# Six projection blocks in seven half-size products, with weight sums added up by loads and scan operands read from DRAM

## The chip, the cores and the metric

The kernel runs on one core of a Trainium2 chip. The metric is the device time of one execution in microseconds: the median of three runs of the kernel before is 1147.17 us (1144.52 to 1148.08).

## The reference

One decoder block works on 1024 tokens of 1024 features, in float32. It normalises the input (`h`), multiplies it by one wide weight `w_in`, and feeds two mixers from the columns of the result.

```
h = _rmsnorm(x, norm_w[layer])
proj = h @ w_in[layer]
dsa_qkv, dsa_z, gdn_qkv, gdn_z, gdn_b, gdn_a, gate_a, gate_b = _split_columns(proj)
y_a = (o_a * jax.nn.silu(dsa_z)) @ w_up_a[layer]
y_b = (o_b * jax.nn.silu(gdn_z)) @ w_up_b[layer]
merged = jax.nn.sigmoid(gate_a) * y_a + jax.nn.sigmoid(gate_b) * y_b
x = x + merged @ w_out[layer]
```

Mixer A is a mixture of three dilated window attentions (`o_a`). Mixer B is a gated delta rule, evaluated in 16 chunks of 64 tokens with a state that is handed from chunk to chunk (`o_b`):

```
v_new = u_c - jnp.einsum('bhck,bhkv->bhcv', w_c, state)
o = jnp.einsum('bhck,bhkv->bhcv', q_e, state) + jnp.einsum('bhij,bhjv->bhiv', at, v_new)
state = state * dec[..., None, None] + jnp.einsum('bhck,bhcv->bhkv', k_d, v_new)
```

A final normalisation follows. `z` (the `dsa_z` and `gdn_z` columns, 512 each) and the gates (1024 each) are plain projections of `h`.

## The kernel before

**Numbers.** Every float32 factor of a projection is held as two float16 parts (`h_hi`, `h_lo`; `whi`, `wlo`), and a product is three matmuls of float16: hi by hi, hi by lo, lo by hi (`mm3_steps`, L150 to L152). A weight block comes from DRAM in float32 (`wstage`, issued by GpSimd's queue, POOL, L132), ScalarE makes the hi part (L136) and VectorE the lo part (`wlo`, in the helper at L62).

**Units and the feed.** The projections are cut into units of 256 columns. A unit is 32 steps of three matmuls with 512 tokens each, in four outputs of 128 columns by 512 tokens. `Feed` holds the units in a row, `feed.tick(n)` writes the next n steps into TensorE's program, and while one unit runs, the weights of the next are loaded (at the start) and split (8 and 14 steps later). All other work of the kernel is written between such ticks, so that TensorE has matmuls to do while other engines prepare.

**Stages.** First `h` is made (to about 60 us), then come the attentions with the q, k and v units between them (to about 565 us), the preparation of mixer B with its units and the triangular solves (to about 790 us), the scan (to about 925 us), the up products and the output product. The solves run on VectorE at low priority, their results go through DRAM (`u_d`, `t_d`) into `MT`, and `merge` needs them.

**The scan.** Its loop (L1194) handles two chunks an iteration. A chunk has three places where TensorE needs VectorE: the state's products (L1212) go to `z` on VectorE, `z` goes into the product with `U` (L1232), its result becomes `vn` on VectorE, and `vn` goes into the state's update (L1241), which VectorE adds to `Sb`. Between them stand 4, 2 and 2 steps of the feed (`PACE`). The units that fill them are the two z units of mixer A, whose results are used at once (`z_now`), the two of mixer B (`z_keep`), and gate unit 6. Gate unit 7 is run after the scan. All operands of the scan but `kdec` lie in SBUF.

**What sets the order.** TensorE's instructions stand in the order in which the code writes them. Those of VectorE, ScalarE and the DMA queues are put in order when the kernel is built, by a scheduler that follows priorities (`tc.high_priority`, with an offset for lower ones); on the chip each engine then works off its list in that order.

## Time and profile before

| | us |
|---|---|
| median of three runs | 1147.17 |
| the profiled execution | 1144.65 |
| its span, from the first to the last instruction | 1142.9 |
| TensorE busy (PE) | 1116.6 |
| VectorE busy (DVE) | 757.9 |
| ScalarE busy (ACT) | 491.7 |

The difference of 1.75 us between execution and span lies outside of the instructions. In the rows, `out<-in` names what is written and read, `x` is a count, and a helper's line stands for all its callers (L62 and L65 are VectorE's, L150 to L152 TensorE's). A row of a timeline begins with the start and the length in us. In a table of windows a row has the stretch, its length, and then the busy time of PE, PEld, DVE, ACT and POOL, the granted clock, the share of the DMA engines and GB/s. A row of the DMA view has the count of loads, the size of one and the median time from issue to landing.

### The profile page before, as it was taken

To read this page: it belongs to the slowest core of one execution; us is meant where nothing else is said; L and a number is where in the kernel's file an instruction comes from. 1 tells how busy PE (TensorE), PEld (TensorE's weight loads), DVE (VectorE), ACT (ScalarE), POOL (GpSimd) and SP (SyncE) were. 2 spreads that over 40 slices of the span, in tenths; PEclk is the share of its full clock that TensorE was granted. 3 is DMA by queue.
4 is the path that set the end of the run, shared out by engine and by line. 5 is a ranking of instruction groups with operands and counts; after the bars stand their busy time and mean duration, and the time that the engine had idled before them with its cause. 6 is when DMAs were issued, how large, how long until landed. Compare 5 with 4: busy or idle time off the path is not lost.

```text
span 1142.9 us, 23354 instructions
## 1 busy us (share of the span) xinstructions
PE 1116.6 (98%) x9410; PEld 672.3 (59%) x9410; DVE 757.9 (66%) x1818; ACT 491.7 (43%) x1128; POOL 57.5 (5%) x103
## 2 busy tenths in 40 slices
PE   6999999999999999999999999999999999999997
PEld 6894775956857655856555544455555544444443
DVE  5775747568577378737977997973776662775223
ACT  6455746466455355446654423442322133331211
POOL 2100000000000000000000000000000000100000
PEclk9999999999999999999999999999999999999999
DMA  7144343413623423333212524242111116540232
GB/s 273 64 139 121 110 119 94 121 57 90 172 75 95 124 76 93 103 103 113 66 38 80 144 96 113 76 82 76 56 57 57 48 56 258 192 140 1 74 111 75
DMA packets 73053, 115.28 MB, mean 101 GB/s; under 512 B 30560, under 2 KB 41184, under 8 KB 72816
## 3 DMA queue, kind: packets, MB, share of 16 engines
q1 hardware_dynamic: 56064, 65.14, 19.7%
q0 software_dynamic: 12128, 44.11, 12.1%
q10 hardware_dynamic: 4752, 4.52, 1.1%
q8 instruction: 74, 1.21, 0.5%
q14 instruction: 35, 0.29, 0.1%
HBM read 73.70 MB, written 21.17 MB: 83 GB/s over the span
## 4 chain that ended last, share of the span: by engine, by line
PE 74%; DVE 18%; DMA 3%; ACT 2%; issue 2%; SPq 1%; DVEq 0%; ACTq 0%
PE ps_mm L150 20%; PE ps_mm L151 19%; PE ps_mm L152 19%; DVE wlo L62 2%; PE ps_G L607 2%; DVE ca L62 2%; DVE X L65 2%; DVE stmp L65 2%; PE ps_S L151 1%; PE ps_S L150 1%; PE ps_S L152 1%; DVE rt L65 1%; PE ps_S L586 1%; PE ps_S L584 1%; DMA og<-og 1%
## 5 line engine op out<-in xcount | busy, mean ns | idle before, releaser
L150 PE MATMUL ps_mm<-h_hi,whi 128*128 128x512 f16 (+1 forms) x912 | 345.1, 378 | 0.1
L151 PE MATMUL ps_mm<-h_lo,whi 128*128 128x512 f16 (+1 forms) x912 | 343.9, 377 | 1.0 <-DVE h_lo L65 1.0
L152 PE MATMUL ps_mm<-h_hi,wlo 128*128 128x512 f16 (+1 forms) x912 | 343.9, 377 | 0.0
L152 PEld LDWEIGHTS <-wlo 128*128 128x128 f16 x1088 | 106.4, 98 | 122.8 <-issue 1.2
L150 PEld LDWEIGHTS <-whi 128*128 128x128 f16 x1088 | 106.3, 98 | 86.3
L151 PEld LDWEIGHTS <-whi 128*128 128x128 f16 x1088 | 106.5, 98 | 79.6 <-issue 0.3
L597 ACT ACTIVATE sm<-sm,osb 128x128 f32<-128x128 f32 (+1 forms) x192 | 85.0, 444 | 91.2 <-DVE osb L593 90.6
L62 DVE SCALAR_TENSOR_TENSOR wlo<-wstage,whi 128x1024 f16<-128x1024 f32 x80 | 97.2, 1222 | 39.5 <-ACT whi L136 39.2
L150 PE MATMUL ps_mm<-whi,h_hi 128*128 128x256 f16 x384 | 105.1, 274 | 0.0
L151 PE MATMUL ps_mm<-wlo,h_hi 128*128 128x256 f16 x384 | 104.7, 273 | 0.1
L152 PE MATMUL ps_mm<-whi,h_lo 128*128 128x256 f16 x384 | 104.7, 273 | 0.0
L136 ACT ACTIVATE whi<-wstage 128x1024 f16<-128x1024 f32 x79 | 82.6, 1054 | 40.4 <-PE ps_mm L151 36.2
L65 DVE TENSOR_TENSOR tl<-ps_G,th 128x256 f16<-128x256 f32 (+1 forms) x96 | 52.1, 543 | 38.6 <-ACT th L612 38.2
L593 DVE CUSTOM_DVE_ANT_0 sm<-ps_S,amask 128x128 f32<-128x128 f32 (+1 forms) x192 | 59.4, 347 | 26.9 <-PE ps_S L586 26.8
L132 POOL DMA_DIRECT2D wstage<-in_w x68 | 36.0, 529 | 784.3 <-DVE wlo L62 594.7
L65 DVE TENSOR_TENSOR rt<-rx,tabs 128x512 f32<-128x512 f32 x96 | 64.9, 687 | 15.4 <-ACT rx L439 14.3
L62 DVE SCALAR_TENSOR_TENSOR ca<-xc,cw,ca 128x512 f32<-128x512 f32 x72 | 53.7, 746 | 2.2 <-ACT ca L793 1.6
L150 PE MATMUL ps_mm<-wo_hi,m_hi 128*128 128x512 f16 (+2 forms) x136 | 49.5, 366 | 0.0
L151 PE MATMUL ps_mm<-wo_lo,m_hi 128*128 128x512 f16 (+2 forms) x136 | 49.5, 366 | 0.0
L152 PE MATMUL ps_mm<-wo_hi,m_lo 128*128 128x512 f16 (+2 forms) x136 | 49.4, 366 | 0.0
L607 PE MATMUL ps_G<-cons,sm 128*128 128x128 f32 x280 | 46.4, 273 | 1.7 <-DVE tl L65 1.6
L151 PEld LDWEIGHTS <-h_hi 128*128 128x128 f16 x384 | 45.8, 119 | 1.3
(273 smaller groups left out, 1856.2 us busy)
## 6 DMA issues: line engine op xcount, KB each, us to landing
wstage<-in_w POOLq DMA_DIRECT2D x68, 512.0 KB, 4.6
og<-osb ACTq DMA_DIRECT2D x32, 132.0 KB, 2.1
og<-og SPq DMA_DIRECT2D x32, 132.0 KB, 2.2
gspa<-gst SPq DMA_DIRECT2D x16, 256.0 KB, 2.1
wstage<-in_w_up POOLq DMA_DIRECT2D x8, 512.0 KB, 5.0
sga<-gspa SPq DMA_DIRECT2D x8, 512.0 KB, 4.9
wstage<-in_w_out POOLq DMA_DIRECT2D x8, 512.0 KB, 4.4
xr<-in_x SPq DMA_DIRECT2D x8, 512.0 KB, 4.2
```

The lines of the kernel that those rows point to most:

```text
L62: (eng or V).scalar_tensor_tensor(out, in0, scalar, in1, op0=op0, op1=op1)
L65: (eng or V).tensor_tensor(out, in0, in1, op)
L132: (eng or nc.gpsimd).dma_start(out=st, in_=src[:, 4 * c:4 * c + 4])
L136: SC.activation(hi[:, 4 * c:4 * c + 4], st, AF.Copy, scale=W_SCALE)
L150: PE.matmul(out, lhsT=wh(k), rhs=mh(k), start=first and i == 0, stop=False, skip_group_check=True)
L151: PE.matmul(out, lhsT=wh(k), rhs=ml(k), start=False, stop=False, skip_group_check=True)
L152: PE.matmul(out, lhsT=wl(k), rhs=mh(k), start=False, stop=last and i == len(ks) - 1, skip_group_check=True)
L584: PE.matmul(out, lhsT=Q[:, hd, qs], rhs=K[:, hd, ks], start=(u == 0), stop=False, skip_group_check=True)
L586: PE.matmul(out, lhsT=Q[:, hd, qs], rhs=Kl[:, hd, ks], start=False, stop=True, skip_group_check=True)
L593: V.tensor_tensor_reduce(P[:, u, :128 * nk], psc[:, u * 256:u * 256 + 128 * nk], mask, -cexp, -NEG, ALU.add, ALU.min, accum_out=osb[:, 256 ...
L597: SC.activation(P[:, u, :128 * nk], P[:, u, :128 * nk], AF.Exp, bias=osb[:, 256 + hd:257 + hd], scale=-1.0, accum_out=osb[:, 260 + hd:261 ...
L607: PE.transpose(pt[:, c:c + 128], P[:, u, i * 128:i * 128 + 128], ident)
```

## The change

Six units are computed in another way: the four z units and the gate units 6 and 7. A unit's weight is 1024 by 256 and its tokens are 1024, so it can be seen as a product of 2 by 2 blocks, with eight products of blocks (512 deep, 128 columns, 512 tokens). The change uses a scheme with seven products of sums of blocks (`seven_products`), so a unit has 28 steps in place of 32.

- **Sums of h.** During the attentions `sums_of_h` makes the four sums of quarters of `h` on VectorE at low priority, using `kT` as scratch, and stores them in DRAM (`hs_d`). Three come back into tiles of their own (`hsum`); the fourth overwrites a quarter of `h` when gate unit 5 is done (`last_sum`).
- **Sums of weights.** Each unit's blocks lie in DRAM 14 times (`w7`). `Seven.load` loads three plain blocks into `wstage` and four into `wsum`, and then adds four, two and one further blocks to the latter with loads that accumulate (`accum_op`). `Seven.split` makes the hi and lo parts, in four parts spread over the unit before.
- **Sums of results.** They are made in PSUM: ScalarE copies a bank into another and the next product goes on top (`seed_y` and the copies beside it). One bank is kept in SBUF (`x7`), and two of the four outputs are that minus a bank, made by one more VectorE operation.
- **Scan operands.** The tiles that the scan reads (`Rv`, `q`, `U`, `at`) are spilled to DRAM when they are ready and read back iteration by iteration. `m`, `wo` and ten gate tiles become six gate tiles with the gates spilled.
- The z and up units are put into the feed earlier in the code, and the four blocks of `w_out` are fetched one in each up unit.

```diff
--- before.py
+++ after.py
+RUNS7 = 28
...
+        def ahead(self, i):
+            if i >= len(self.units):
+                return
+            at, busy, src = RUNS7 - self.left, self.seven(i - 1), self.units[i][1]
+            if not self.seven(i):
+                if not busy:
+                    self.prefetch(i, FETCH if self.left > FETCH[1] else None)
+                elif at == 1:
+                    with tc.high_priority():
+                        self.st = [load_w(src, c) for c in range(2)]
+                elif at == 17:
+                    self.w[i] = unit_tiles()
+                elif at in (18, 21):
+                    self.split(self.st[at // 21], *self.w[i], at // 21)
+            elif not busy:
+                at += RUNS - RUNS7
+                if at == 0:
+                    src.load()
+                elif at in (12, 18):
+                    src.split(at // 18)
+            elif at == 1:
+                src.load()
+            elif at in (9, 17, 25):
+                src.split(at // 8 - 1)
...
+                if self.seven(i):
+                    src = self.units[i][1]
+                    for n in range(4):
+                        src.split(n)
+                    self.cur, self.left = self.units[i][2](src.blocks), RUNS7
...
+    class Seven:
+        PAIRS = (((0, 0), (1, 0)), ((1, 2), (0, 1)), ((1, 1), (0, 2)), ((1, 3),))
+        def __init__(self, i):
+            self.src, self.blocks, self.loaded, self.split_done = A["w7"][i], [], False, 0
+        def load(self):
+            if self.loaded:
+                return
+            self.loaded = True
+            dma = nc.gpsimd.dma_start
+            with tc.high_priority():
+                self.st = [wst.tile([128, 4, 256], F32, name="wstage", tag="wstage", bufs=2)
+                           .rearrange("p a b -> p (a b)").rearrange("p (s n) -> p s n", n=512) for _ in range(2)]
+                sums = w7pool[0].tile([128, 4, 512], F32, name="wsum", tag="wsum", bufs=1)
+                dma(out=sums, in_=self.src[:, 3:7])
+                dma(out=self.st[0], in_=self.src[:, 0:2])
+                dma(out=self.st[1][:, 0:1], in_=self.src[:, 2:3])
+                dma(out=sums, in_=self.src[:, 7:11], accum_op=ALU.add)
+                dma(out=sums[:, 2:4], in_=self.src[:, 11:13], accum_op=ALU.add)
+                dma(out=sums[:, 3:4], in_=self.src[:, 13:14], accum_op=ALU.add)
+            self.sums = sums
+        def split(self, n):
+            if n < self.split_done:
+                return
+            self.load()
+            self.split_done = n + 1
+            t = w_tile(("whi", "wlo")[n % 2]).rearrange("p k c -> p (k c)").rearrange("p (b l n) -> p b l n", l=2, n=512)
+            for b, (kind, j) in enumerate(self.PAIRS[n]):
+                st = self.sums[:, j] if kind else self.st[j // 2][:, j % 2]
+                SC.activation(t[:, b, 0], st, AF.Copy, scale=W_SCALE)
+                STT(t[:, b, 1], st, W_SCALE, t[:, b, 0], ALU.mult, ALU.subtract)
+                self.blocks.append([t[:, b, x].rearrange("p (k c) -> p k c", c=128) for x in (0, 1)])
...
+    def seven_products(blocks, out):
+        x, q = bank("mm", 3), bank("mm", 3)
+        def product(n, p, first=False):
+            hi, lo = mov7[n]
+            w = blocks[n]
+            return mm3_steps(p, (lambda k: w[0][:, k], lambda k: w[1][:, k]), (hi, lo), ks=range(4), first=first)
+        def then(steps, fn):
+            for i, _ in enumerate(steps):
+                if i == 3:
+                    with tc.high_priority():
+                        fn()
+                yield
+        y, rest = [], []
+        def seed_y():
+            y.append(bank("mm", 3))
+            SC.copy(y[0], x)
+        def keep():
+            rest.append(w7pool[1].tile([128, 512], F32, name="x7", tag="x7", bufs=1))
+            SC.copy(rest[0], q)
+        yield from then(product(0, x, True), seed_y)
+        yield from then(product(1, q, True), keep)
+        yield from then(product(2, x), lambda: SC.copy(q, x))
+        yield from then(product(3, y[0]), lambda: out(0, 0, y[0], None))
+        yield from then(product(4, q), lambda: out(1, 1, q, rest[0]))
+        yield from then(product(5, x), lambda: out(1, 0, x, rest[0]))
+        yield from then(product(6, q), lambda: out(0, 1, q, None))
...
+        if rest is not None:
+            STT(t, p, -1.0, rest, ALU.mult, ALU.subtract)
+            p = t
...
+    def sums_of_h(k):
+        def halves(x):
+            return [x[:, :512], x[:, 512:]]
+        wk = [kT[2 * (k % 2) + i].rearrange("p c i -> p (c i)") for i in range(2)]
+        for i in range(2):
+            TT(wk[i], h_hi[:, 4 * i + k], h_lo[:, 4 * i + k], ALU.add)
+        (x11, x12), (x21, x22) = halves(wk[0]), halves(wk[1])
+        TT(x11, x11, x12, ALU.subtract)
+        TT(x12, x22, x12, ALU.subtract)
+        STT(x22, x22, -1.0, x11, ALU.mult, ALU.subtract)
+        STT(x21, x22, -1.0, x21, ALU.mult, ALU.subtract)
+        for i in range(2):
+            hl = ap.tile([128, 2, S], F16, name="hl", tag="hl", bufs=1)
+            SC.copy(hl[:, 0], wk[i])
+            TT(hl[:, 1], wk[i], hl[:, 0], ALU.subtract)
+            nc.sync.dma_start(out=hs_d[i, :, :, k], in_=hl)
...
+        if sets.index(s) < 4:
+            with tc.high_priority(offset=-SOLVE_LATER):
+                sums_of_h(sets.index(s))
...
-                    TT(Rv[:, t0:t0 + 4, h0:h0 + 2], p.rearrange("p (t h v) -> p t h v", t=4, v=64),
+                    TT(rv, p.rearrange("p (t h v) -> p t h v", t=4, v=64),
                        bc(beta[:, t0:t0 + 4, h0:h0 + 2], 64), ALU.mult)
+                nc.sync.dma_start(out=rv_d[t0:t0 + 4, :, h0:h0 + 2].rearrange("t p h v -> p t h v"), in_=rv)
...
+                  lambda c, q, hb=hb: nc.sync.dma_start(out=q_d[2 * hb + c], in_=q))
...
+        i = 2 * (br == "b") + u
+        feed.add(("z", br, u), Seven(i), gen)
+    def z_silu(out, p, rest):
+        fp = late[0]
+        th = fp.tile([128, 512], F32, name="zt", tag="zt", bufs=1)
+        if rest is not None:
+            STT(out, p, -1.0, rest, ALU.mult, ALU.subtract)
+            p = out
+        SC.activation(th, p, AF.Tanh, scale=0.5 * P_SCALE)
+        STT(out, th, 1.0, p, ALU.add, ALU.mult)
...
+    for i in (6, 7):
+        gate_unit(i, gate_spill, i - 2)
...
+    def spill(x, hb, src):
+        for t0 in (0, 4):
+            nc.sync.dma_start(out=ua_d[x][hb][:, t0:t0 + 4],
+                              in_=src[hb][:, t0:t0 + 4].rearrange("p t e q i -> p t (e q i)"))
+    h = (h_hi, h_lo)
+    hsum = {}
+    def load_sums():
+        for n, (i, c) in ((1, (0, 1)), (2, (1, 1)), (5, (1, 0))):
+            hsum[n] = [fp.tile([128, 4, 512], F16, name=f"hsum{n}", tag="big", bufs=6) for _ in range(2)]
+            for x in range(2):
+                nc.sync.dma_start(out=hsum[n][x], in_=hs_d[i, :, x, :, 512 * c:512 * c + 512])
+    def last_sum():
+        for x in range(2):
+            nc.gpsimd.dma_start(out=h[x][:, 0:4, 512:1024], in_=hs_d[0, :, x, :, 0:512])
...
+        for n, q in ((0, (0, 0)), (3, (4, 0)), (4, (0, 512)), (6, (4, 512))):
+            mov7[n] = quarter_of(*q)
+        for n, tl in hsum.items():
+            mov7[n] = [lambda k, x=x: x[:, k] for x in tl]
+    feed.after["gate", 5] = last_sum
...
+        rvt = cp.tile([128, 8, 64], F32, name="rvt", tag="rvt", bufs=2)
+        nc.sync.dma_start(out=rvt, in_=rv_d[t])
+        U = cp.tile([128, 2, 2, 2, 64], F32, name="U", tag="U", bufs=2)
+        at = cp.tile([128, 2, 2, 2, 64], F32, name="at", tag="at", bufs=AT)
         kdec = cp.tile([128, 8, 64], F32, name="kdec", tag="kdec", bufs=2)
+        qt = cp.tile([128, 4, 2, 64], F32, name="qt", tag="qt", bufs=2)
+        for hb in range(2):
+            nc.sync.dma_start(out=U[:, hb].rearrange("p e q i -> p (e q i)"), in_=ua_d[0][hb][:, t])
         nc.sync.dma_start(out=kdec, in_=kd_d[t])
+        nc.sync.dma_start(out=qt, in_=q_d[:, :, 2 * t:2 * t + 2].rearrange("c p s i -> p c s i"))
+        for hb in range(2):
+            nc.sync.dma_start(out=at[:, hb].rearrange("p e q i -> p (e q i)"), in_=ua_d[1][hb][:, t])
...
+    NR = 6
+    for dt in range(8):
+        for br in "ab":
+            if len(sig) == NR:
+                feed.until(("gate", 7))
+            sig[br, dt] = fp2.tile([128, S], F32, name=f"sg{br}{dt}", tag="sg2", bufs=NR)
+            nc.sync.dma_start(out=sig[br, dt], in_=gsp[br, dt])
...
+    order = "11 12 22  11 21 11 11  21 22 21 21  22 22  12".split()
+    return np.stack([blk[n] for n in order], axis=1)
```

Three places of the engines' lists. First POOL, where the loads of the third such unit (the first z unit of mixer B, z2) are issued while the second runs; `wsum` is the tile of sums, and in brackets is what an instruction waits for:

```order
L302 DMA wstage<-in_w 128x1024 [waits DMASW7_49,DVE_49]
L303 DMA wstage<-in_w 128x512 [waits DMASW0_49,DMASW2_49,DVE_49,Activation_49]
L301 DMA wsum<-in_w 128x2048 [waits DMASW1_49,DMASW6_49,DVE_49,Activation_49]
L304 DMA wsum<-in_w 128x2048 [waits DMASW1_49]
L305 DMA wsum<-in_w 128x1024 [waits DMASW2_49]
L306 DMA wsum<-in_w 128x512 [waits DMASW3_49]
```

Before, there were two loads of 128x1024 for a unit. Now the plain blocks come first, the load of the sums waits for VectorE (the last split of the unit before), and each of the three that accumulate waits for the one ahead of it.

Second VectorE in the scan, in the second unit. A piece of the list before, with a split of a weight:

```order
L65 TENSOR_TENSOR vn<-ps_O,rks 128x256 [waits PE_49]
L65 TENSOR_TENSOR Sb<-Sb,ps_G 128x128 [waits DVE_49,PE_49]
L65 TENSOR_TENSOR Sb<-Sb,ps_G 128x128 [waits PE_49]
L62 SCALAR_TENSOR_TENSOR wlo<-wstage,whi 128x1024 [waits DMASW7_49,PE_49,Activation_49]
L62 SCALAR_TENSOR_TENSOR zs<-zt,ps_mm 128x512 [waits Activation_49]
L65 TENSOR_TENSOR z<-ps_S,bgks 128x2x64 [waits PE_49] x2
```

And the place now where the first sum of z2 is split:

```order
L65 SCALAR_TENSOR_TENSOR whi<-wstage,whi 128x512 [waits DMASW7_49,PE_49,Activation_49]
L68 TENSOR_TENSOR vn<-ps_O,rks 128x256 [waits PE_49]
L68 TENSOR_TENSOR Sb<-Sb,ps_G 128x128 [waits DVE_49,PE_49]
L68 TENSOR_TENSOR Sb<-Sb,ps_G 128x128 [waits PE_49]
L65 SCALAR_TENSOR_TENSOR whi<-wsum,whi 128x512 [waits DMASW2_49,Activation_49]
L68 TENSOR_TENSOR z<-ps_S,bgks 128x2x64 [waits PE_49] x2
```

The split of 1024 elements has become splits of 512, and the one of a sum stands between `Sb` and `z` of the scan and waits, through DMASW2, for the first load that accumulates.

Third SP, the queue of the DMAs around the second solve (`u_d` and `t_d` take its results, `MT` and `T1p` are loaded for the second merge). Before:

```order
L1033 DMA u_d_9040<-X 128x1024 [waits DMAHW1_49,DVE_49,Pool_49]
L1034 DMA t_d_9041<-T_9038 128x1024 [waits DMAHW2_49,DVE_49]
L1046 DMA MT_8034<-u_d_9040 32x32x32 [waits DMAHW3_49,DMAHW1_49]
L1044 DMA T1p<-t_d_9041 32x32x32 [waits DMAHW4_49,DMAHW2_49,PE_49]
L1046 DMA MT_8034<-u_d_9040 32x32x32 [waits DMAHW5_49]
L1044 DMA T1p<-t_d_9041 32x32x32 [waits DMAHW6_49]
```

Now:

```order
L1185 DMA u_d_9111<-X 128x1024 [waits DMAHW4_49,DVE_49,Pool_49]
L1186 DMA t_d_9112<-T_9109 128x1024 [waits DMAHW5_49,DVE_49]
L1198 DMA MT_8090<-u_d_9111 32x32x32 [waits DMAHW6_49,DMAHW4_49]
L1196 DMA T1p<-t_d_9112 32x32x32 [waits DMAHW7_49,DMAHW5_49,PE_49]
L1264 DMA q_d<-qT_8092 128x1024 [waits DMAHW0_49,DVE_49]
L1357 DMA a_d_8101<-E_8087 128x1024 [waits DMAHW1_49,DVE_49]
L1198 DMA MT_8090<-u_d_9111 32x32x32 [waits DMAHW2_49]
L1196 DMA T1p<-t_d_9112 32x32x32 [waits DMAHW3_49]
L1357 DMA a_d_8101<-E_8087 128x1024 [waits DVE_49]
L1264 DMA q_d<-qT_8093 128x1024 [waits DVE_49]
L1198 DMA MT_8090<-u_d_9111 32x32x32 [waits DMAHW6_49]
```

Spills of `qT` and of `E` (`a_d`) have come in among the loads of `MT` and `T1p`.

264 lines of the change are left out of this document (142 added, 122 removed).

## The prediction

> **What bounds the kernel now.** I read the page first, then the TensorE rows one by one in a quiet stretch, then the busy time stage by stage, and last the loads.
>
> ```profile
> span 1142.9 us, 23354 instructions
> PE 1116.6 (98%) x9410; PEld 672.3 (59%) x9410; DVE 757.9 (66%) x1818; ACT 491.7 (43%) x1128; POOL 57.5 (5%) x103
> PEclk9999999999999999999999999999999999999999
> PE 74%; DVE 18%; DMA 3%; ACT 2%; issue 2%; SPq 1%; DVEq 0%; ACTq 0%
> ```
>
> TensorE is busy 98% of the span at full clock and holds 74% of the chain that ended last. A matmul that goes therefore gives back time, if nothing else comes to stand in front of TensorE. But not its listed length: the rows overlap. The first and the last of 36 matmuls in a row, in the timeline of TensorE:
>
> ```profile
> 924.76 0.39 PE L150 MATMUL ps_mm<-h_hi,whi 128*128 128x512 f16 x1
> 932.33 0.38 PE L152 MATMUL ps_mm<-h_hi,wlo 128*128 128x512 f16 x1
> ```
>
> They start 7.57 us apart over 35 steps, 0.216 us each. I price a 128x512 matmul at 0.216 us and not at 0.38. The stages, from the table of windows (span, then busy PE, PEld, DVE, ACT, POOL):
>
> ```profile
> 100.00:440.00 340.00, 340.00 (x2732) 230.68 (x2731) 222.09 (x607) 193.28 (x528) 14.79 (x28) 1.00 0.35 101
> 565.00:700.00 135.00, 130.45 (x918) 70.71 (x919) 111.56 (x241) 56.59 (x102) 7.74 (x15) 1.00 0.35 95
> 800.00:835.00 35.00, 35.00 (x440) 18.50 (x438) 24.94 (x62) 13.84 (x19) 1.58 (x3) 1.00 0.19 58
> 835.00:870.00 35.00, 34.86 (x459) 18.42 (x458) 27.01 (x69) 8.61 (x13) 1.05 (x2) 1.00 0.18 58
> ```
>
> In the scan (from about 790 to 925 us) TensorE hardly ever waits, VectorE is 71 to 77% busy, and the DMA engines stand at a share of 0.18. Everything this change adds there must fit under TensorE.
>
> **What is removed.** Six units have 28 steps of three matmuls where they had 32: 6 x 12 = 72 matmuls, 72 x 0.216 = 15.6 us. All lie in a stretch where TensorE sets the pace, so without a new wait the time falls by 15.6 us. That is the lower bound of the result: 1144.65 (the profiled execution; its span is 1142.9, with 1.75 around it) - 15.6 = 1129.
>
> **What is added, in the order of its weight.** *The accumulating loads.* How a scan step goes, in the timelines of TensorE and of POOL's loads:
>
> ```profile
> 854.46 0.46 PE L1212 MATMUL ps_S<-Sb,kT 64*64 64x64 f32 x16
> 857.78 0.79 PE L1232 MATMUL ps_O<-z,MT 64*64 64x64 f32 x16
> 859.90 0.46 PE L1241 MATMUL ps_G<-vn,kdec 64*64 64x64 f32 x16
> 862.57 0.27 PE L1212 MATMUL ps_S<-Sb,kT 64*64 64x64 f32 x2
> 832.98 0.53 POOL L132 DMA_DIRECT2D wstage<-in_w  x1 [27.00 <-DVE wlo L62]
> 864.19 0.53 POOL L132 DMA_DIRECT2D wstage<-in_w  x1 [23.56 <-DVE wlo L62]
> ```
>
> A unit of 32 steps took 31.2 us, so a step of the feed costs 0.975 us with the scan's share, a chunk of the scan 7.8 us, and a new unit of 28 steps 27.3 us. In it four loads must follow one another into one tile: 1 MB plain, then 1 MB, 512 KB and 256 KB added on, each issued by POOL when the one before has landed. The tile is free only when the unit before has split its last sum; the sums of the first unit, z0, are loaded long before the scan, so z1, z2, z3, gate 6 and gate 7 are left.
>
> VectorE works off its list in order, and the list is fixed (the rows shown with the change). For unit z2 the last split of z1's sums stands four operations behind the `vn` of a second chunk, some 3.1 us after the L1232 row. The split of z2's first sum, which needs the first accumulation, stands just ahead of `z` two chunks on. From L1232 to that L1212 are 862.57 - 857.78 = 4.8 us and a first chunk of 15.6 - 8.1 = 7.5 us, 12.3 in all. `z` may come about 1.3 us late before its matmul (3.3 us behind L1212) waits, and starts 0.5 us after L1212; ScalarE's and VectorE's split with their hand-offs cost 1.6. So the load may land 12.3 + 0.5 + 1.3 - 1.6 - 3.1 = 9.4 us after the tile is free. The same counting gives 11.3, 9.4, 13.4, 12.3 and 12.0 us for z1, z2, z3, gate 6 and gate 7, and 13.7, 14.1, 16.8 and 16.3 us to the second accumulation in the first four.
>
> How long the loads take, from the DMA view of 800 to 925 us:
>
> ```profile
> q0 software_dynamic: 1152, 4.19, 10.2%
> wstage<-in_w POOLq DMA_DIRECT2D x8, 512.0 KB, 4.0
> kdec<-kd_d SPq DMA_DIRECT2D x6, 256.0 KB, 2.7
> ```
>
> 4.19 MB in 10.2% of 125 us are 328 GB/s while packets move, so 512 KB are 1.6 us of moving and 2.4 us of the rest, and 1 MB lands in 5.6 us. No row shows an accumulating load. **From below** it costs what a plain load does: 0.2 + 5.6 + 0.3 + 5.6, and 0.5 for sharing with the scan's own loads, is 12.2 us to the first accumulation and 16.5 to the second. Against the windows that is late by 2.8, 2.8, 0, 0.2 and 0.2 us: 6 us. **From above**, an addition needs the old value as well as the new, so the moving part may be twice as long (8.8 and 5.6 us): 15.4 and 21.3, with 0.5 more for the longer sharing 21.8. That is late by 8.1, 7.7, 5.0, 5.5 and about 4 us: 30 us. I take the middle, one and a half times the moving part (7.2 and 4.8 us), 13.8 and 18.9 us to the two accumulations: late by 5.2, 4.8, 2.1, 2.6 and 2, together **16.7 us**. What is late then: VectorE stands at the split, behind it are `z` or `vn` of the scan, for these TensorE waits, and all feed matmuls behind them.
>
> [...]
>
> That such splits are placed too early for real loads can be seen in before, in the stage of the up products, where it costs nothing since TensorE has other work:
>
> ```profile
> ACT wo_hi L136 <- DMA wstage<-in_w_out: 20.2, 8, 4.6
> ```
>
> ScalarE waited there 2.5 us on average at each of eight splits. That speaks for lateness.
>
> *VectorE in the scan.* A unit now has seven splits of 512 instead of two of 1024, and two more operations that negate and subtract the kept half:
>
> ```profile
> L62 DVE SCALAR_TENSOR_TENSOR wlo<-wstage,whi 128x1024 f16<-128x1024 f32 x9 | 11.0, 1222 | 7.6 <-ACT whi L136 7.5
> L62 DVE SCALAR_TENSOR_TENSOR zs<-zt,ps_mm 128x512 f32<-128x512 f32 x8 | 5.5, 685 | 6.6 <-ACT zt L1158 6.4
> ```
>
> 7 x 0.69 - 2 x 1.22 + 2 x 0.69 = 3.8 us more in 27.3, and the unit's own twelve operations of 0.68 come in 27.3 and not 31.2 us. From 77% this goes to about 94% in the two units of mixer A, to some 80% in those of B. Price 1 us (0 to 4). ScalarE gains about as much and stays near half busy: nothing.
>
> *The sums of h.* Four times four passes over 1024 and four over 512 elements on VectorE: 4 x (4 x 1.22 + 4 x 0.69) = 31 us in the attention, where it is busy 222 of 340 us and these come at low priority. Hidden; 1 us (0 to 3).
>
> *Spills ahead of the second merge.* In before TensorE waits almost nothing for the solved blocks:
>
> ```profile
> PE ps_O L1070 <- DMA MT<-u_d: 0.4, 1, 0.4
> ```
>
> On SP, between the loads of the second `MT` there now stand two stores of `a_d` and two of `q_d`, which wait for VectorE. 0.4 us of wait means that there is no slack: a store costs SP about 0.6 us to issue, so 2 us (0 to 5).
>
> *The scan's operands from DRAM.* They come a whole iteration ahead (15.6 us against 2.7 for 256 KB): nothing. Only the first set has no lead. Its `rvt` and `U` are issued once the last reads of the old tiles are over, and 18 matmuls, 3.9 us, stand before the first use: 1 us (0 to 3). The six loads of summed h and the overwrite of a quarter of h lie before their products or 16 steps ahead of them; the copies that seed a bank have four steps, 2.6 us without the scan, for 0.6 us of ScalarE: nothing.
>
> **The sum.** 1144.65 - 15.6 + 16.7 + 1 + 1 + 2 + 1 = 1150.8 for an execution like the profiled one. That one was 2.5 us below the median of the runs, 1147.17, so I add half of this and forecast 1152 us, five more than before.
>
> **The rivals.** *Accumulating is no dearer than a plain load.* For it: the windows for z3, gate 6 and gate 7 are then met as they stand. Against: z2's 9.4 us are short for two loads of 5.6 one after the other. 1144.65 - 15.6 + 6 + 3 = 1138, in the runs about 1139 to 1141: faster. *The addition doubles the moving.* 30 us in place of 16.7: 1164, about 1166 in the runs, slower by 1.6%. For it: the old tile must be read as well as the new block. Against: the two reads may overlap. [...] *The chain of loads becomes the bound of the unit.* If adding is three times as slow in its moving part (12.0, 7.2, 4.8 us), the four loads with hand-offs take 0.2 + 5.6 + 12.0 + 7.2 + 4.8 + 0.9 + 1.6 for the last split = 32.3 us, more than a unit's 27.3; the second accumulation comes at 26.1 us, and the lateness is 12.4, 12.0, 9.3, 9.8 and about 8, 51 us: 1185. It decides from the point where the four loads no longer fit in 27 us. *VectorE is the bound in mixer A's units:* at 94% a queue may delay each of seven chunks by its 0.6 us; with plain loads that is 4 us more than I priced, about 1144, no change.
>
> **How the numbers follow.** My forecast 0.38, plain loads 0.26, VectorE with plain loads 0.06, doubled 0.20, load-bound 0.10. A difference under 0.3% (3.4 us: 1143.7 to 1150.6) can't be told from none. Faster: nearly all of the plain case and the low end of mine, where the splits turn out to stand a little later than I counted, 0.33. Within: the rest of the plain case, the VectorE case and some of mine, 0.16. Slower: 0.51. The range of 8 in 10 reaches from 1136 (plain loads with the small terms at their low ends) to 1176 (doubled, with the small terms at their high ends); my forecast's own range is 1144 to 1161.
>
> **What would show it.** Right: among TensorE's waits, VectorE's `z`, `vn` or `Sb` with several us each, four or five times some 30 us apart, and ScalarE waiting on the loads of `wsum` just before; the first accumulating 1 MB landing in about 7 us. Wrong: those loads landing in under 6 us and TensorE without a wait from 790 to 945 us; then the time falls to about 1140. Over 8 us means the doubled case. A wait of TensorE for `MT<-u_d` of more than 5 us or a slower attention stage (before 440 us) would show one of the small terms mis-sized.

## The result, and the profile after

The changed kernel takes 1207.51 us (median; 1204.95 to 1211.18), the kernel before 1146.43 us beside it: 1.0536 times as long, with a 95% interval from 1.0499 to 1.0573. The forecast was 1152 us, its range ended at 1176. The profiled execution is 66.5 us longer than that of before (spans 1209.4 and 1142.9).

The page of the changed kernel, the rows that answer to those of before (span, busy times, granted clock in 40 slices, chain of waits):

```profile
span 1209.4 us, 23586 instructions
PE 1127.1 (93%) x9338; PEld 675.2 (56%) x9338; DVE 802.4 (66%) x1892; ACT 519.6 (43%) x1184; POOL 78.2 (6%) x129
PEclk9998999999999999999999989998988888999999
PE 51%; DVE 21%; DMA 14%; issue 7%; ACT 4%; SPq 2%; POOL 1%; DVEq 0%; ACTq 0%; POOLq 0%
```

TensorE's share of the chain fell from 74 to 51%, VectorE and the loads came in. The third row is the surprise. Before it was a row of nines; now there are dips, most of them in the scan. Its mean, by the view of the cores, is 0.973, and 0.999 before.

What TensorE waits for in the changed kernel (us in total, times, longest):

```profile
PE ps_O L1470 <- DVE z L68: 21.8, 7, 6.6
PE ps_G L427 <- DVE xt L65: 7.7, 1, 7.7
PE ps_S L705 <- DMA Kl<-pkB: 6.5, 2, 4.1
PE ps_G L1490 <- DVE Sb L68: 5.2, 1, 5.2
PE ps_mm L156 <- ACT ps_mm L352: 4.4, 1, 4.4
PE ps_O L1470 <- DMA U<-u_d: 4.1, 1, 4.1
PE ps_S L1205 <- DMA T1p<-t_d: 3.5, 1, 3.5
PE ps_S L705 <- DMA Kl<-pcBl: 3.5, 2, 2.1
PE ps_O L1470 <- ACT z L1465: 3.0, 1, 3.0
PE ps_S L156 <- DVE sga L65: 2.8, 1, 2.8
```

The wait for `xt` stands at the very start, and before has it too (7.8 us). Of the others before had only one above 1 us, 1.7 us for `Kl`. ScalarE's waits for `wsum`, which the prediction named as the sign, are there too, five of them at the first sum of a unit:

```profile
ACT whi L317 <- DMA wsum<-in_w: 35.8, 5, 9.2
```

The stages in the table of windows (columns as before), at the same times as in the prediction, so that the scan has only begun in the third row:

```profile
100.00:440.00 340.00, 330.10 (x2620) 223.36 (x2621) 223.97 (x584) 189.88 (x509) 13.74 (x26) 0.98 0.38 112
565.00:700.00 135.00, 132.39 (x941) 73.71 (x940) 115.85 (x277) 61.85 (x125) 10.21 (x18) 1.00 0.41 112
800.00:835.00 35.00, 27.87 (x322) 15.86 (x319) 10.41 (x23) 9.95 (x21) 2.92 (x5) 0.92 0.82 276
835.00:870.00 35.00, 29.14 (x319) 14.12 (x318) 22.01 (x53) 12.29 (x20) 3.70 (x5) 0.88 0.68 174
```

In the scan VectorE is far from full (22.0 of 35 us), the DMA engines went from a share of 0.18 to 0.68 and 0.82, and the clock is 0.88 to 0.92.

**One stall, row by row.** The unit z2 is split while z1 runs. In the timelines of POOL, ScalarE and VectorE of the changed kernel (start, length, in brackets the idle time before and what ended it):

```profile
870.74 0.53 POOL L301 DMA_DIRECT2D wsum<-in_w  x1 [4.81 <-DVE Sb L68]
877.39 0.87 POOL L304 DMA_DIRECT2D wsum<-in_w  x1 [6.12 <-DMA wsum<-in_w]
885.78 0.85 POOL L305 DMA_DIRECT2D wsum<-in_w  x1 [7.52 <-DMA wsum<-in_w]
885.51 0.63 ACT L317 ACTIVATE whi<-wsum 128x512 f16<-128x512 f32 x1 [7.94 <-DMA wsum<-in_w]
886.17 0.69 DVE L65 SCALAR_TENSOR_TENSOR whi<-wsum,whi 128x512 f16<-128x512 f32 x1 [7.69 <-ACT whi L317]
886.78 0.48 DVE L68 TENSOR_TENSOR z<-ps_S,bgks 128x128 f32<-128x128 f32 x2
```

The plain 1 MB took 6.65 us to the next issue, the first accumulating 1 MB 8.39. ScalarE stood 7.94 us at the split, VectorE 7.69 us behind it, and `z` of the scan came next on VectorE's list. TensorE in the same place:

```profile
882.30 0.38 PE L158 MATMUL ps_mm<-h_hi,whi 128*128 128x512 f16 x1
888.07 0.45 PE L1470 MATMUL ps_O<-z,U 64*64 64x64 f32 x2 [5.39 <-DVE z L68]
890.89 0.63 PE L158 MATMUL ps_mm<-h_hi,whi 128*128 128x512 f16 x1
891.32 0.63 PE L156 MATMUL ps_mm<-hsum,whi 128*128 128x512 f16 x1
894.52 0.38 PE L156 MATMUL ps_mm<-hsum,whi 128*128 128x512 f16 x1
894.74 0.38 PE L157 MATMUL ps_mm<-hsum,whi 128*128 128x512 f16 x1
```

It waits 5.39 us. Then it goes on at half speed: 0.43 us from matmul to matmul until 894.4, and only then 0.22 again. The windows around it show the granted clock (last but two columns):

```profile
880.70:884.20 3.50, 1.98 (x10) 0.69 (x7) 0.00 (x0) 0.00 (x0) 0.00 (x0) 1.00 1.00 207
884.20:887.60 3.40, 0.00 (x0) 0.00 (x0) 1.39 (x5) 1.63 (x3) 0.85 (x1) 1.00 0.54 115
887.60:894.40 6.80, 5.83 (x41) 2.91 (x42) 4.86 (x11) 1.14 (x2) 0.84 (x1) 0.50 0.79 168
894.40:901.00 6.60, 6.60 (x101) 3.84 (x99) 6.50 (x15) 3.53 (x6) 0.56 (x1) 1.00 0.62 179
```

A stretch without a matmul, then 6.8 us at a clock of 0.50. The ten dips within the work of the changed kernel are of this kind. In the clock records of its trace they start whole multiples of 3.413 us apart and last 3.413, 6.827 or 10.240 us, that is one, two or three slots of such a grid. Each stands behind a slot in which TensorE was held up and worked 0.00 to 0.39 of the time.

**A ledger.** For every run I added up, over TensorE's rows, the time between the end of one matmul and the start of the next (waits), and half of the time that it worked at a clock of 0.50 (lost to the clock; in the rows above 0.43 us from matmul to matmul in place of 0.22). What is left of the span is the work itself with its first and last microseconds. Where two of these kernels are some 5 us apart or less, their intervals overlap, and the difference is uncertain.

| kernel | median us | ratio to before (95%) | span | waits | lost to the clock | rest |
|---|---|---|---|---|---|---|
| before | 1146.4 | | 1142.9 | 12.3 | 0.0 | 1130.6 |
| the changed kernel | 1207.5 | 1.0499 to 1.0573 | 1209.4 | 68.4 | 23.4 | 1117.6 |
| `plain_loads` | 1180.4 | 1.0277 to 1.0323 | 1182.6 | 46.3 | 17.4 | 1118.9 |
| `one_load` | 1169.5 | 1.0176 to 1.0236 | 1173.5 | 43.4 | 11.7 | 1118.4 |
| `h_sums_later` | 1208.4 | 1.0509 to 1.0567 | 1208.1 | 67.8 | 22.4 | 1117.9 |
| `h_sums_gated` | 1203.1 | 1.0457 to 1.0512 | 1201.6 | 65.1 | 20.3 | 1116.2 |
| `start_ticks` | 1202.4 | 1.0448 to 1.0512 | 1200.1 | 65.0 | 16.1 | 1119.0 |
| `own_chains` | 1189.8 | 1.0315 to 1.0418 | 1189.7 | 55.8 | 15.3 | 1118.6 |
| `all_mends` | 1186.7 | 1.0303 to 1.0364 | 1185.0 | 54.5 | 14.1 | 1116.4 |
| `sums_ahead` | 1173.0 | 1.0195 to 1.0245 | 1176.0 | 46.4 | 8.9 | 1120.7 |
| `ahead_mends` | 1170.1 | 1.0178 to 1.0218 | 1167.3 | 38.0 | 12.3 | 1117.0 |
| `ahead_spread` | 1165.1 | 1.0103 to 1.0184 | 1164.6 | 34.7 | 13.1 | 1116.8 |
| `graded_stalls` | 1219.7 | 1.0617 to 1.0660 | 1218.1 | 56.5 | 23.1 | 1138.5 |

The last column of all kernels with the change lies between 1116 and 1121, 10 to 14 us below before. The 72 matmuls are gone and worth about what they should be. The whole loss is in the two columns ahead of it: 56 us of waits more, and 23 us of clock.

### The profile page after: what moved, and what is told of

It reads as the page before. It is cut to its first block, busy times and chain, and to the rows that moved or that the text cites. A ratio compares the mean times of both kernels' runs of the same rounds, so it can differ in the third digit from the quotient of the medians.

```text
span 1209.4 us, 23586 instructions
## 1 busy us (share of the span) xinstructions
PE 1127.1 (93%) x9338; PEld 675.2 (56%) x9338; DVE 802.4 (66%) x1892; ACT 519.6 (43%) x1184; POOL 78.2 (6%) x129
## 4 chain that ended last, share of the span: by engine, by line
PE 51%; DVE 21%; DMA 14%; issue 7%; ACT 4%; SPq 2%; POOL 1%; DVEq 0%; ACTq 0%; POOLq 0%
PE ps_mm L156 13%; PE ps_mm L157 13%; PE ps_mm L158 13%; DMA wsum<-in_w 8%; DVE wlo L65 3%; DVE ca L65 2%; PE ps_G L726 2%; SPq L585 2%; DVE stmp L68 1%; DVE X L68 1%; DMA wstage<-in_w 1%; DVE sm L712 1%; PE ps_S L156 1%; DVE tl L68 1%; PE ps_S L158 1%
## 5 line engine op out<-in xcount | busy, mean ns | idle before, releaser
L156 PE MATMUL ps_mm<-h_hi,whi 128*128 128x512 f16 (+1 forms) x768 | 293.6, 382 | 4.5 <-ACT ps_mm L352 4.4
L157 PE MATMUL ps_mm<-h_lo,whi 128*128 128x512 f16 (+1 forms) x768 | 292.9, 381 | 1.0 <-DVE h_lo L68 1.0
L158 PE MATMUL ps_mm<-h_hi,wlo 128*128 128x512 f16 (+1 forms) x768 | 291.2, 379 | 0.0
L158 PEld LDWEIGHTS <-wlo 128*128 128x128 f16 x968 | 95.4, 99 | 110.8 <-issue 5.0
L157 PEld LDWEIGHTS <-whi 128*128 128x128 f16 x992 | 97.9, 99 | 81.3 <-issue 11.7
L156 PEld LDWEIGHTS <-whi 128*128 128x128 f16 x992 | 97.7, 98 | 80.4 <-issue 4.9
L65 DVE SCALAR_TENSOR_TENSOR wlo<-wstage,whi 128x1024 f16<-128x1024 f32 x68 | 82.5, 1220 | 16.4 <-ACT whi L139 16.4
L139 ACT ACTIVATE whi<-wstage 128x1024 f16<-128x1024 f32 x67 | 69.6, 1053 | 17.7 <-PE ps_mm L157 9.6
L68 DVE TENSOR_TENSOR rt<-rx,tabs 128x512 f32<-128x512 f32 x96 | 65.1, 687 | 9.0 <-ACT rx L558 8.2
L156 PE MATMUL ps_mm<-wo,mhi 128*128 128x512 f16 (+2 forms) x136 | 49.5, 366 | 0.0
L157 PE MATMUL ps_mm<-wo,mhi 128*128 128x512 f16 (+2 forms) x136 | 49.5, 366 | 0.0
L158 PE MATMUL ps_mm<-wo,mlo 128*128 128x512 f16 (+2 forms) x136 | 49.4, 366 | 0.0
L705 PE MATMUL ps_S<-Kl,Qs 128*128 128x128 f16 (+1 forms) x192 | 39.5, 245 | 9.9 <-DMA Kl<-pkB 6.5
```

The costliest lines, as they stand in the source:

```text
L65: (eng or V).scalar_tensor_tensor(out, in0, scalar, in1, op0=op0, op1=op1)
L68: (eng or V).tensor_tensor(out, in0, in1, op)
L139: SC.activation(hi[:, 4 * c:4 * c + 4], st, AF.Copy, scale=W_SCALE)
L156: PE.matmul(out, lhsT=wh(k), rhs=mh(k), start=first and i == 0, stop=False, skip_group_check=True)
L157: PE.matmul(out, lhsT=wh(k), rhs=ml(k), start=False, stop=False, skip_group_check=True)
L158: PE.matmul(out, lhsT=wl(k), rhs=mh(k), start=False, stop=last and i == len(ks) - 1, skip_group_check=True)
```

## The experiments

### Adding taken out of the loads

```diff
-                dma(out=sums, in_=self.src[:, 7:11], accum_op=ALU.add)
-                dma(out=sums[:, 2:4], in_=self.src[:, 11:13], accum_op=ALU.add)
-                dma(out=sums[:, 3:4], in_=self.src[:, 13:14], accum_op=ALU.add)
+                dma(out=sums, in_=self.src[:, 7:11])
+                dma(out=sums[:, 2:4], in_=self.src[:, 11:13])
+                dma(out=sums[:, 3:4], in_=self.src[:, 13:14])
```

> The changed kernel with its three accumulating loads of a unit made plain loads of the same size, in the same order and with the same waits (the sums of the weights are then not made, so the output isn't the reference's). Changed kernel: 1207.5 us; its first accumulating 1 MB took 8.4 to 10.5 us to the next issue, the 512 KB 5.7 to 6.1. Theory A (the price of adding is what was mis-sized): those fall to about 6.5 and 4.5 us, the first sum comes some 3 us earlier in each of five units, the stalls of the scan (33 us) shrink by about 15 us and the half-clock time behind them with it: 1180 to 1192 us. Theory B (the chain of loads is too long whatever the loads do): 1198 to 1208. Theory C (adding is all of it): under 1170.

1180.36 us, 27 less than the changed kernel. The same four loads in POOL's timeline:

```profile
862.29 0.53 POOL L301 DMA_DIRECT2D wsum<-in_w  x1 [4.82 <-DVE Sb L68]
869.15 0.53 POOL L304 DMA_DIRECT2D wsum<-in_w  x1 [6.32 <-DMA wsum<-in_w]
874.74 0.53 POOL L305 DMA_DIRECT2D wsum<-in_w  x1 [5.06 <-DMA wsum<-in_w]
878.84 0.54 POOL L306 DMA_DIRECT2D wsum<-in_w  x1 [3.57 <-DMA wsum<-in_w]
```

The second 1 MB takes 5.59 us in place of 8.39, 0.35 of it because POOL's issue is shorter (0.53 and 0.88 us). The loads of the first unit, far ahead of the scan and at the same place in both kernels, show the same: 8.34 us (594.28 to 602.62) and 5.55 (594.80 to 600.35). TensorE's waits for `z` fall from 21.8 to 9.7 us:

```profile
PE ps_O L1470 <- DVE z L68: 9.7, 6, 3.2
```

Theory A holds, at the low end of its range: 3 to 4 us less in the first of these loads and 1 to 2 in most of the second ones, in five units, are worth 22 us of waits and 6 us of clock.

### The three loads left out

```diff
-                dma(out=sums, in_=self.src[:, 7:11], accum_op=ALU.add)
-                dma(out=sums[:, 2:4], in_=self.src[:, 11:13], accum_op=ALU.add)
-                dma(out=sums[:, 3:4], in_=self.src[:, 13:14], accum_op=ALU.add)
```

> The changed kernel with the three accumulating loads of a unit left out, so that each unit has its one plain 1 MB load of sums and the plain blocks (the sums of the weights are not made, so the output isn't the reference's). Theory A and B alike (late sums stall VectorE, and with it TensorE): 47 us go, 33 of stalls and 14 of the half-clock time behind them: 1155 to 1170 us, and no wait of TensorE for z over 2 us in the scan. Rival (VectorE's longer list of splits is the bound, the loads only lie beside it): above 1190.

1169.48 us: the chain as a whole costs 38 us. Two of TensorE's waits in this kernel:

```profile
PE ps_O L1467 <- DMA U<-u_d: 4.5, 1, 4.5
PE ps_O L1467 <- DVE z L68: 3.4, 3, 2.7
```

VectorE still has all its seven splits a unit, and `z` is late by 3.4 us in all (one wait of 2.7, over the 2 that was expected at most; it stands behind a split for whose plain load ScalarE waited 5.5 us). So a longer list on VectorE is a small matter; a list that stands still at a load is the large one. But the kernel is still 23 us slower than before, which the chain does not explain.

### The sums of h, moved twice

The first edit puts the sums of `h` beside the last attentions in the code:

```diff
-        if sets.index(s) < 4:
+        if sets.index(s) >= 3:
             with tc.high_priority(offset=-SOLVE_LATER):
-                sums_of_h(sets.index(s))
+                for k in (0, 1):
+                    sums_of_h(2 * (sets.index(s) - 3) + k)
```

> The changed kernel with the four sums of h moved from the first to the last attentions (two with the fourth, two with the fifth set). In the changed kernel the first two sets lose 15.3 us against before: 9.9 us of waits for Kl and about 4 us at half clock. Theory (VectorE, ScalarE and the loading queue have no room beside the first two sets): those waits go back to 1.7 us, 1207.5 - 14 = 1193 (1188 to 1200). Rival (the waits come from the other order of the loads of Qs and Ks, whoever has the work): 1203 to 1211.

1208.40 us, no change, though not for the reason that the rival names. VectorE's timeline of this kernel:

```profile
52.24 1.22 DVE L68 TENSOR_TENSOR kT<-h_hi,h_lo 128x1024 f32<-128x1024 f16 x1
53.38 0.68 DVE L68 TENSOR_TENSOR ro<-rt,rt 128x512 f32<-128x512 f32 x1
```

The sums start at 52 us, as in the changed kernel (51.6 us). Their priority is low, but their operands are ready at once, and the scheduler put them into the first gap that it saw. The experiment had moved nothing, so it told nothing. The second edit adds a dependence:

```diff
+        for i in range(2):
+            SC.copy(wk[i][:, 0:1], after[:, 7, 0:1])
         for i in range(2):
             TT(wk[i], h_hi[:, 4 * i + k], h_lo[:, 4 * i + k], ALU.add)
```

> The changed kernel with the sums of h moved again to the fourth and fifth set of the attentions, and this time held there: their scratch is first touched by a one-column copy of the values of that set, which exist only then. (Moving them in the code alone had left them on the same place of VectorE's list, since the scheduler fills gaps with whatever is ready.) Theory (VectorE, ScalarE and the loading queue have no room beside the first two sets): the waits for Kl fall from 9.9 to 1.7 us and the half-clock time there goes: 1207.5 - 14 = 1193 (1188 to 1199). Rival (something else of the change delays the first sets): 1203 to 1211.

Now the sums lie at 334 to 426 us. 1203.10 us, 4 less where 14 were expected. In the first two sets the theory holds. The matmul that starts at 163.5 us in before (L586, now L705) comes 14.0 us later in the changed kernel and 4.6 us later here, and what is left of the waits for `Kl` is

```profile
PE ps_S L705 <- DMA Kl<-pkB: 2.5, 1, 2.5
PE ps_S L705 <- DMA Kl<-pcBl: 1.7, 1, 1.7
```

But beside the later sets VectorE isn't free either: at 476 us of before the lateness is 7.4 us, where it is 16.0 in the changed kernel. Part of the gain was given back. The profiled executions differ by 7.8 us and the medians by 4.4, so part of what is missing is scatter between executions. The wait for `T1p` is 4.9 us here and 3.5 in the changed kernel, but between 2.7 (`h_sums_later`) and 6.2 (`start_ticks`) in other runs, so it tells nothing here.

Why there was no room beside the first set can be read in the queue of SP: in the changed kernel the loads of `Kl` are

```profile
92.62 4.97 SPq L585 DMA_DIRECT2D Kl<-pkA  x8
97.70 7.45 SPq L585 DMA_DIRECT2D Kl<-pkB  x8
```

and in before

```profile
87.24 6.33 SPq L466 DMA_DIRECT2D Kl<-pkA  x8
94.07 5.43 SPq L466 DMA_DIRECT2D Kl<-pkB  x8
```

Each sum of `h` stands on VectorE among the operations that make `pkA` and `pkB` (`rt`, `ro`), and the first set of the attentions can't begin before them. VectorE's 65% over the stage hide that it has no gap at all there: in the timeline of before, none from 44 to 76 us.

### Stalls of known length in the kernel before

```diff
+    def stall(k):
+        p = bank("O", 1)
+        with tc.high_priority():
+            PE.matmul(p[:, :64], lhsT=ident, rhs=ident[:, :64], start=True, stop=True, skip_group_check=True)
+            SC.copy(idle[:, :64], p[:, :64])
+            for _ in range(k):
+                SC.activation(idle, idle, AF.Copy)
+            PE.matmul(p[:, :64], lhsT=ident, rhs=idle[:, :64], start=True, stop=True, skip_group_check=True)
```

> The kernel before with 12 artificial stalls of TensorE in the up products and the output product: TensorE waits for a chain of 2 to 9 dependent ScalarE copies of 512 elements, about 1.5 to 6 us each. In the changed kernel the granted clock falls to one half on a fixed grid of 3.413 us, after a slot in which TensorE was busy less than 0.40 of the time (never after one with 0.45 or more), and comes back after a slot that is full. Theory: stalls under 2 us never lower the clock, those over 4.1 us always do, those between do by where they fall in the grid; a lowered clock lasts 1 or 2 slots more and costs 1.7 to 3.4 us on top. Rival (the clock falls for another reason that the scan has, such as the loads): no half clock in this kernel, and the time grows by the sum of the stalls alone.

The stalls became 1.3 to 8.4 us long, from the start of one matmul to the start of the next. The clock fell behind nine of them, all from 2.6 us up, and behind none of the three at 1.28, 1.29 and 2.42 us. One of these three, and the longest, in TensorE's timeline:

```profile
1118.78 0.43 PE L1347 MATMUL ps_O<-idle,cons 128*128 128x64 f32 x2 [2.15 <-ACT idle L1346]
1024.93 0.69 PE L1347 MATMUL ps_O<-idle,cons 128*128 128x64 f32 x2 [8.12 <-ACT idle L1346]
```

and the windows at the longest:

```profile
1015.80:1019.20 3.40, 1.01 (x6) 0.58 (x4) 1.85 (x3) 2.91 (x5) 0.33 (x1) 1.00 0.11 43
1019.20:1029.40 10.20, 4.47 (x12) 1.99 (x13) 6.14 (x7) 4.64 (x7) 1.79 (x4) 0.50 0.60 205
```

The slot to 1019.20 has 1.01 us of work in 3.40; the next three run at half. In this kernel nothing but the stalls was added, so the clock fell behind TensorE's standing still alone, without anything that the scan does. The nine stalls cost 23.1 us on top of themselves, 2.6 us each.

The bound that I had read from the changed kernel alone, that the clock never falls behind a slot with 0.45 of work, is wrong. Over all runs of this study the clock fell behind 81 slots. All slots that the clock records show at full clock with less than 0.43 of work are among them, none with more than 0.53, and between these both occur; my share of work within a slot is worked out from modelled ends of matmuls and may be off by a little.

So in these runs the work in a slot told whether the clock fell, and the length of one wait did not. In `ahead_spread`, the last run below, the clock fell five times though no wait within its work is over 2.44 us. At one of these places, with the wait and the windows:

```profile
489.78 0.66 PE L738 MATMUL ps_G<-cons,sm 128*128 128x128 f32 x4 [1.96 <-DVE tl L68]
487.40:490.80 3.40, 1.44 (x13) 1.15 (x12) 3.19 (x14) 2.73 (x11) 0.00 (x0) 1.00 0.55 144
490.80:494.20 3.40, 3.40 (x26) 2.52 (x25) 2.78 (x7) 0.32 (x1) 0.00 (x0) 0.50 0.41 96
```

The three stalls without a dip above left their slots 0.78, 0.70 and 0.55 full. When the clock came back is less clear. In the changed kernel each dip ended with its first slot that was 0.94 or more full; in the first merge of `all_mends` (711.0 to 721.3 us) the clock stayed at 0.50 for three slots that the windows show as full of work, a part of it matmuls of 32 by 32. Why is open.

### A chain for each of the four sums

`wsum` is cut into four tiles of 256 KB. Each has loads of its own and is loaded again as soon as its own split is done, one unit earlier:

```diff
+        STAGES = (((0, 0),), ((2, 0), (0, 1)), ((1, 0), (2, 1)), ((3, 0), (2, 2), (1, 1)), ((3, 1),), ((3, 2),), ((3, 3),))
+        def advance(self, n):
+            with tc.high_priority():
+                while self.stage < n:
+                    for j, x in self.STAGES[self.stage]:
```

> The changed kernel with the tile of four weight sums cut into four tiles with a chain of loads each (same bytes, same SBUF); a tile's next chain begins when its own split is done, one unit earlier, and the loads that follow one another are issued some 8 steps apart. The first sum of a unit then has some 27 us in place of some 9 to 13. Theory (late loads are all that stalls the scan): the stalls at z, vn and Sb in the five units and the half-clock time behind them go, as in the kernel with one plain load (1169.5): 1163 to 1176 us, though every addition is made. Rival (VectorE's seven splits a unit, or twice as many loads on POOL's queue, take their place): above 1185.

1189.77 us, between the changed kernel and `one_load`, and in the range of the rival. Eleven loads of 256 KB stand on POOL's list in place of four, and the scheduler put most of the additions right behind the load that they add to:

```profile
POOL wsum L312 <- DMA wsum<-in_w: 121.2, 33, 8.3
ACT wlo L335 <- DMA wsum<-in_w: 26.4, 4, 9.5
```

These are 33 waits of 3.7 us in one queue. A quarter of the bytes did not take a quarter of the time (from issue to landing 5.0 us in the median, against 8 to 10 for the accumulating 1 MB of the changed kernel), and late sums still hold up ScalarE, by 26.4 us in four waits. So I read the rows as POOL's queue being the bound in place of the tile; no run shows the queue by itself. Its price is what I had left out.

### More cover at the start of the scan, and all mends together

```diff
-            feed.tick(PACE[0])
+            feed.tick(PACE[0] if ch else 12)
```

> The changed kernel with 12 in place of 4 steps of the feed ahead of the scan's first product with U, 5.2 us more of TensorE's work while the first operands come from DRAM. In the changed kernel this product waits 3.0 us for z and 4.1 us for U, and 10 us run at half clock. Theory: 5.2 of the 7.1 us go, and most of the half clock, about 5 us on top: 1197 to 1204. Rival (the feed's work is moved only, and the units behind get less time for their loads): 1205 to 1211.

1202.39 us, as expected, 5 less (the two intervals just overlap); the wait for `U` falls from 4.1 to 1.8 us. But where the changed kernel's z1 waited 4.9 us, one wait for `z` now takes 9.4. The steps that were moved ahead of the scan run there without the scan's share, so z1's loads get fewer microseconds to the same step. The rival is right too, in part.

The next run has this edit, the two of `h_sums_gated` and `own_chains`, and the loads of the solved blocks put first:

```diff
+        with tc.high_priority():
             for kb in range(4):
                 b = kb % 2
                 if b == 0:
                     nc.sync.dma_start(out=T1p[32 * kb:32 * kb + 32].rearrange("p t h j -> p (t h) j"),
```

> The three changes of this call together (own chains, held sums of h, 12 steps ahead of the scan), and the loads of the solved blocks (MT, T1p) put ahead of other traffic of their queue. If the four places are independent: 1207.5 less about 38 (chains), 14 (sums of h), 7 (start of the scan) and 5 (merge), 1143 us, about the kernel before (1137 to 1150). If the half size products are worth their 15.6 us once nothing waits: down to 1132.

1186.72 us, where 1143 was hoped for. Alone, three of the mends had given 17.7, 4.4 and 5.1 us, 27.2 together; here all four give 20.8. The lateness of the attentions is nearly gone (2.5 us at 431 us of before, 3.7 at 541), that of the scan is not: of the 54.5 us of waits that remain 27.5 lie in its five units, two of them 9.1 and 8.1 us long. So the mends don't add up. VectorE's list is made anew for each kernel, and the late splits come to stand before other operations; that this is the reason is a reading of the rows, not shown by a run.

### Finished sums

The weight sums depend on no data of the kernel. Here the same additions are made from DRAM to DRAM beside the attentions, and the scan loads 1 MB of sums, plain:

```diff
+    ws_d = [tc.dram_tile([128, 4, 512], F32, name=f"ws_d{i}") for i in range(6)]
+    def weight_sums(u, after):
...
+        for n, (c, k) in enumerate(((0, 3), (0, 7), (2, 11), (3, 13))):
+            for i in u:
+                src = A["w7"][i][:, k:k + 4 - c]
+                if n:
+                    nc.gpsimd.dma_start(out=ws_d[i][:, c:4], in_=src, accum_op=ALU.add)
+                else:
+                    nc.gpsimd.dma_start(out=ws_d[i], in_=src)
...
-                dma(out=sums, in_=self.src[:, 3:7])
+                dma(out=sums, in_=ws_d[self.i])
```

> The changed kernel with the weight sums of all six units made long before they are needed: during the attentions (one unit with each set from the second on, held there by a few elements that are written first) the same loads, one plain and three accumulating, go from DRAM to DRAM, and in the scan a unit loads its 1 MB of finished sums in one plain load. Theory (it is the chain's place beside the scan that costs, not the additions as such): the scan goes as in the kernel with one load (1169.5 us), and the output is now the reference's: 1163 to 1178 us. Rival (four loads that wait for one another keep POOL's queue from the attention's weight loads, some 25 us a unit): waits for wlo or whi in the attentions, above 1185.

1173.01 us, with all the arithmetic of the change, and the scan goes as in `one_load`. TensorE's longest waits are elsewhere now; the largest of the attentions is

```profile
PE ps_O L765 <- DVE tl L68: 6.6, 3, 4.2
```

at 538 and 555 us, where the sums of two units are made behind one another and POOL's weight loads wait. The rival is there, but small.

Then with the mends of `all_mends` but its chains, and

```diff
-                    feed.fetch(A["w_out"][u], [wo16[0][:, :, us], wo16[1][:, :, us]], (14, 22))
+                    feed.fetch(A["w_out"][u], [wo16[0][:, :, us], wo16[1][:, :, us]], (18, 26))
```

> The same with the sums of h held to the fourth and fifth set, 12 steps of the feed ahead of the scan's first product, the loads of MT and T1p put first in their queue, and the splits of w_out four steps later. The profiled execution of the kernel with one load still lost some 15 us in the attentions, 8 in the first merge, 11 at the start of the scan, 7 between scan and up products. If they can be had one by one: 1169.5 - 35 = 1135 (1130 to 1142), below the kernel before. If VectorE's or the queues' order only moves the waits to other places, as the four mends together did before (1186.7 where 1143 was hoped for): 1150 to 1175.

1170.09 us: three us for four mends. The same wait (`tl`) is now one of 6.7 us. The last run makes these two units' sums one by one in mixer B's preparation:

```diff
-    weight_sums((4, 5), tiles[sets[-1]][3])
...
         feed.until(("gdn", hb, 1))
+        weight_sums([4 + hb], kT[2 * hb], gs)
```

> The kernel with finished sums and all the mends (1170.1 us), with the sums of the last two units made one after the other in mixer B's preparation in place of both together with the last set of the attentions, where TensorE waited 6.9 us at once and ran 6.8 us at half clock. Its trace has 38.0 us of TensorE's waits and 12.3 us lost at half clock; before has 12.3 and none. Theory (each place where four loads follow one another takes POOL's queue from the weight loads; one unit at a time is short enough): some 12 us go, 1155 to 1161. Rival (the same wait comes back in the preparation): 1165 to 1174.

1165.14 us, on the edge between both expectations. None of its waits within the work is over 2.44 us, and still it has 34.7 us of them and 13.1 us of clock, so it is 1.4% slower than before. No version here beats the kernel before.

## Why the prediction was wrong

Its direction was right, and so were the mechanism and the place: VectorE at the split, `z`, `vn` or `Sb` behind it, ScalarE waiting for `wsum`, five times some 30 to 40 us apart. The size was not: +66 us in the profiled executions, where its sum had +6. By its own steps:

| step of the prediction | forecast | waits measured | lost to the clock |
|---|---|---|---|
| 72 matmuls removed (last column of the ledger) | -15.6 | -13.0 | |
| lateness in z1, z2, z3, gate 6, gate 7 | 16.7 | 33.4 | 13.7 |
| the sums of h | 1 | 8.2 more than before | 3.9 |
| spills ahead of the merge | 2 | 3.5 | 2.8 |
| first scan operands | 1 | 7.1 | 3.1 |
| the up products | not named | 2.8 | |

Together -13.0 + 55.0 + 23.5 = 65.5, and the spans differ by 66.5. The waits of a row are TensorE's idle times at that place, the last column is half of its work in the slots at half clock behind them.

**The step that failed first is the price of the accumulating loads**, "one and a half times the moving part (7.2 and 4.8 us)". To the next issue the 1 MB took 8.4 to 10.5 us in the five units (mean 9.4), the plain 1 MB ahead of it 6.2 to 8.1. From the issue of the plain load to the split of the first sum, which starts when that sum has landed, are 18.1, 14.8, 15.8, 16.4 and 15.5 us; the forecast had 13.8, its upper end 15.4. To the split of the second sum are 24.1, 20.5, 21.6, 22.5 and 25.0 us, forecast 18.9 and at the upper end 21.8. Two things are in this. Adding nearly doubled the moving here: against `plain_loads` 8.39 to 5.59 us, and less the 2.4 us of the rest (my estimate from the rows of before) 6.0 to 3.2. That was the rival of the doubled moving, which I gave 0.20. And the loads were slower in the scan than in the quiet rows that I took 5.6 us from (median to landing: 512 KB of `wstage` 4.4 us in place of 4.0, 256 KB of `kdec` 5.0 in place of 2.7, the plain 1 MB of the five units 7.2), while the change raised the DMA share of the scan from 0.18 to about 0.7. I allowed 0.5 us for that. That the share is the reason was not tested by itself.

With these times, the prediction's own windows (11.3, 9.4, 13.4, 12.3, 12.0 us to the first sum, 13.7, 14.1, 16.8, 16.3 to the second, the later of the two deciding) give 10.4, 6.4, 4.8, 6.2 and 3.5 us, 31.3 in all, close to the 33.4 of the table. So the windows were about right together and the loads were mis-sized. Unit by unit TensorE waited 4.9, 5.9, 5.8, 7.2 and 9.6 us. z1 waited less than its window says; its loads were issued at 827.3 us, before the scan's start had finished waiting (833.7). Gate 7 waited more: 4.4 us for a copy on ScalarE (L352) that stood behind the split that waited, and 5.2 for `Sb` behind the second accumulation, whose window I had not counted there. "ScalarE gains about as much and stays near half busy: nothing" is thus wrong too. ScalarE stands at the same load as VectorE.

**The step that was missing is the clock.** The prediction took every stall at its own length. In this kernel each of the ten dips behind a stall costs 1.6 to 3.1 us on top, 23.4 us in all, more than the 16.7 us that the lateness grew by. The kernel before could not show it: its longest time from one matmul's start to the next within the work was 2.2 us, and none of its slots there was less than half full (the emptiest 0.52, on the grid of the one dip at its very end).

**"Hidden; 1 us (0 to 3)" for the sums of h** went by VectorE's share of the whole stage, 222 of 340 us. The scheduler didn't place them in the stage, but at its very beginning, where VectorE has no gap. `h_sums_gated` shows that they are the cause of most of it: the lateness of 14.0 us at 163.5 us fell to 4.6.

**"Only the first set has no lead ... 1 us"** for the first operands: they are issued within some 5 us together with the first tiles of the second set and with 1.25 MB of z1's loads, at a DMA share of 0.82, and TensorE got `U` 7.3 us after the first of its two issues (826.45 to 833.71).

**Spills, 2 us (0 to 5):** the wait is within the range but stands at the first merge and not at the second. There the second load of `T1p` is issued 7.0 us after the first (703.03, 710.01), with stores of `rv_d` and `gspb` between them; in before 1.0 us after it. **VectorE in the scan, 1 us (0 to 4):** `one_load` doesn't contradict it; `z` waits 3.4 us there, 2.7 of them for a load. **The up products** were not named: 2.8 us for `sga`, whose cause no run here isolates.

Of the rivals the one that the chain of loads binds the unit (1185, chance 0.10) came nearest to the time, and not by its mechanism: the unit z2's loads took some 25 us, less than the 27.3 of a unit. The doubled moving was right in its mechanism and nearly in its lateness (30 us, measured 33.4); its sign, over 8 us for the accumulating 1 MB, is there, with 8.1 to 10.2 us from issue to split. Its 1166 us is too low by the clock, which it left out, and by the sums of `h` and the scan's first operands, which it priced at 1 us each. The range should have been open upward, as every term was priced by a single number while VectorE, ScalarE, SP and POOL each work off one list in order, where late things pass their lateness on (ScalarE's 7.94 us at a load, in the rows above, were 7.69 on VectorE and 5.39 on TensorE).
